# Row means of 16384 rows on one core: how many loads stand ahead of the opening barrier, and which wait the last store carries

## The chip, the core and the metric

The kernel runs on one core of a Trainium2 chip. A core has five engines with an instruction queue each. Four of them matter here: VectorE (DVE in the profile), ScalarE (ACT), GpSimd (POOL) and SyncE (SP), which in this kernel issues every DMA and computes nothing. Sixteen DMA engines move the data; one `dma_start` on 128 partitions is spread over all of them. The engines run on their own and meet only at semaphores. The metric is the device time of one execution in microseconds; lower is better.

## The reference

```
x = np.random.randn(32, 512, 1024).astype(np.float32)
out = (np.sum(x, axis=-1) / 1024.0).astype(np.float32)      # (32, 512)
```

Each of the 32 x 512 = 16384 rows of 1024 numbers is summed and divided by 1024. The input is 67.1 MB, the output 65.5 KB.

## The kernel before

**Tiling.** The 16384 rows are dealt to 128 partitions, 128 rows to each. A partition's rows are in three parts: the first F = 15 rows of the tensor's front (`x_first`), and then M = 97 main rows (`x_main`) and L = 16 last ones (`x_last`), which lie one after the other. One row on all partitions is 128 x 1024 float32, 512 KB.

**Loads.** The list `loads` is made at L99 to L107 and has ten entries, numbered k = 0 to 9 here. Their rows are 2, 16, 16, 16, 16, 16, 15 (main), 15 (first), 10 and 4 (last). Two more DMAs, `pa` and `pb` (L140, L141), bring the last two rows of each partition in unequal halves. Load k goes to buffer `bulk[k % 3]`, of 16 rows each, so there are three buffers, and load k can't be issued before load k - 3 has been consumed.

**The opening.** At L110 the first three loads, which wait for nothing, are issued by SP. `start_loads_at_once` (L15) runs when the program is put together: it takes SP's leading DMAs that carry no wait out of the body and puts them in the first block, ahead of the instruction (a Drain) with which SP joins the first barrier. L113 and L114 close the tile context, and there all engines meet again. Until that barrier opens, no engine gets to the kernel's own instructions, which lie behind a branch (L242).

**The body.** From L130 on SP goes through the other loads in order. Ahead of each it waits until VectorE (`by_dve`), ScalarE (`by_act`, where it has a share) and the earlier load into the same buffer are done (L134 to L137). It then issues the two halves of the last rows and the stores of `res` and `res0` (L143, L145), for which GpSimd has to scale the sums first (L152, L156). VectorE sums whole loads with one `reduce_sum` each (L189); of the loads for the last rows it sums row by row (L180). ScalarE takes 4, 6, 4 and 1 rows of the last four loads and the first row of `pa` (L164).

**The end.** SP waits for VectorE's count and ScalarE's count (L203, L204), and stores the last sums, `fin` (L205). Then it waits for the two other stores, clears the semaphores, and waits for the last store to land (L211). Of the two waits ahead of the last store one is an instruction of its own, and the other is carried by the DMA instruction: in the program before, SP first waits for ScalarE alone, and the store carries the wait for VectorE.

Of the kernel before, what the change touches and what calls it, by code (L numbers as in the profile page):

```python
# [35 lines left out]
def kernel(  # L36
# [6 lines left out]
    nc = tc.nc  # L43
# [36 lines left out]
    loads = []  # L80
    sems = {}

    def sem(name):
        sems[name] = nc.alloc_semaphore(name)
        return sems[name]
# [4 lines left out]
    dve, act, pool = sem("by_dve"), sem("by_act"), sem("by_pool")  # L90
# [8 lines left out]
    for part, src, dst, by in (  # L99
# [3 lines left out]
        for rows, on_act in part:  # L103
            t, s, slot = bulk[n % 3][:, :rows, :], in_bulk[n % 3], n
# [2 lines left out]
            j += rows  # L107


    for t, s, src, *_ in loads[:3]:  # L110
        i = nc.sync.dma_start(out=t, in_=src).then_inc(s, 16)  # L111
        tc.no_tile_sem_insts.add(i.ins.name)
    tc.close()  # L113
# [14 lines left out]


    for k, (t, s, src, on_act, dst, by, slot) in enumerate(loads):  # L130
        if k < 3:
            continue
        if slot is not None:
            nc.sync.wait_ge(dve, done_dve[k - 3])  # L134
            if done_act[k - 3]:
                nc.sync.wait_ge(act, done_act[k - 3])
            nc.sync.wait_ge(s, arrived[k] - 16)  # L137
        nc.sync.dma_start(out=t, in_=src).then_inc(s, 16)  # L138
# [10 lines left out]
    k = len(main) - 1  # L149
# [9 lines left out]
    a = 0  # L159
# [40 lines left out]
    d += 1  # L200


    nc.sync.wait_ge(dve, d)  # L203
    nc.sync.wait_ge(act, a)  # L204
    nc.sync.dma_start(out=o_last, in_=fin).then_inc(landed, 16)  # L205
    for s in (out_first, out_main):
        nc.sync.wait_ge(s, 16)
# [39 lines left out]
```

## Time and profile before

| what | value |
|---|---|
| device time, median of 3 runs (lowest, highest) | 160.44 us (160.39, 160.65) |
| the profiled execution: its own time | 160.87 us |
| the profiled execution: its span | 159.5 us |
| bytes moved, mean rate over the span | 67.18 MB, 421 GB/s |
| DMA queue's time, as a share of 16 engines' span | 98.1% |
| VectorE busy | 116.6 us (73%) |
| ScalarE busy | 18.5 us (12%) |
| GpSimd busy | 1.0 us |

The span runs from the first instruction of the profiled execution, which is SP's first DMA issue, to the last. The 1.4 us between the span and the execution's own time lie outside the kernel's instructions. A DMA packet is counted in the stretch in which it starts, so in short stretches the DMA's rate can read zero while all 16 engines are in the middle of a packet. The waits that end idle time are worked out from semaphore events.

### The profile page before, as it was taken

How to read it: one execution, taken by the hardware profiler on the slowest of the kernel's cores; microseconds unless marked ns; L12 is line 12 of the kernel's file. 1: busy time of each engine (PE TensorE's matmuls, PEld its weight loads, DVE VectorE, ACT ScalarE, POOL GpSimd, SP SyncE). 2: the span in 40 equal slices, each digit the busy share in tenths (PEclk: the TensorE clock that was granted, in tenths of full speed). 3: DMA queues.
4: the chain of work that ended last, by engine and by line, in shares of the span. 5: the costliest groups of instructions: out<-in, count | busy, mean ns of one | idle time of the engine just before them, and what ended most of it. 6: DMA issues, size and time to landing. Idle time of an engine off the chain costs nothing.

```text
span 159.5 us, 141 instructions
## 1 busy us (share of the span) xinstructions
DVE 116.6 (73%) x30; ACT 18.5 (12%) x33; POOL 1.0 (1%) x7
## 2 busy tenths in 40 slices
DVE  0500009999499994999949998599979990399475
ACT  3000000000000000000000000000009100392384
POOL 0000000000000000000000000000000001000000
DMA  8996996996996996998969969998997999798994
GB/s 310 479 526 279 509 526 263 526 526 263 526 526 263 526 493 296 526 427 361 526 296 493 526 263 526 493 385 354 493 493 308 431 493 493 329 462 359 423 396 150
DMA packets 2160, 67.18 MB, mean 421 GB/s; under 512 B 624, under 2 KB 624, under 8 KB 880
## 3 DMA queue, kind: packets, MB, share of 16 engines
q1 hardware_dynamic: 2160, 67.18, 98.1%
HBM read 67.11 MB, written 0.07 MB: 421 GB/s over the span
## 4 chain that ended last, share of the span: by engine, by line
DMA 67%; DVE 29%; another core or an unknown queue 1%; ACT 1%; SPq 1%; issue 0%
DMA bulk<-in_x_dram 52%; DVE res L189 29%; DMA pa<-in_x_dram 15%; ACT junk L164 1%; SPq L111 1%; SPq L138 0%
## 5 line engine op out<-in xcount | busy, mean ns | idle before, releaser
L189 DVE TENSOR_REDUCE res<-bulk 128x16 f32<-128x16384 f32 (+3 forms) x8 | 110.0, 13753 | 37.8 <-DMA bulk<-in_x_dram 37.8
L164 ACT ACTIVATE junk<-bulk 128x1024 f32<-128x1024 f32 x15 | 15.2, 1012 | 136.4 <-DMA bulk<-in_x_dram 136.4
L180 DVE CUSTOM_DVE_ANT_0 bulk<-bulk 128x512 f32<-128x512 f32 x9 | 5.7, 689 | 3.4 <-DMA bulk<-in_x_dram 3.4
L164 ACT ACTIVATION_READ_ACCUMULATOR junk<-bulk 128x1 f32 x15 | 2.8, 186 | 0.0
L164 ACT ACT_TABLE_LOAD x1 | 1.3, 1283 | 2.4 <-PEq L114 2.4
L152 POOL TENSOR_SCALAR res<-res 128x97 f32<-128x97 f32 x1 | 0.5, 467 | 129.3 <-DVE res L189 129.3
L164 ACT ACTIVATE junk<-pa 128x1024 f32<-128x1024 f32 x1 | 1.0, 1028 | 0.7 <-DMA pa<-in_x_dram 0.7
L180 DVE DVE_READ_ACCUMULATOR2_ANT fin<- 128x1 f32 x10 | 0.8, 83 | 0.0
L180 DVE CUSTOM_DVE_ANT_0 pb<-pb 128x257 f32<-128x257 f32 x1 | 0.4, 428 | 0.3 <-DMA pb<-in_x_dram 0.3
L180 DVE CUSTOM_DVE_ANT_0 pa<-pa 128x256 f32<-128x256 f32 x1 | 0.4, 424 | 0.0
L156 POOL TENSOR_SCALAR res<-res 128x15 f32<-128x15 f32 x1 | 0.3, 264 | 15.7 <-DVE res L189 15.7
L164 ACT ACTIVATION_READ_ACCUMULATOR junk<-pa 128x1 f32 x1 | 0.2, 186 | 0.0
L148 POOL MEMSET pb<- 128x2 f32 x1 | 0.1, 99 | 2.0 <-POOLq L114 2.0
L228 POOL MEMSET const-bfloat16-1.0<- 128x1 bf16 x1 | 0.1, 101 | 0.0
L228 POOL MEMSET const-uint8-127<- 128x1 uint8 x1 | 0.1, 101 | 0.0
L228 POOL MEMSET const-float32-0.0<- 128x1 f32 x1 | 0.1, 99 | 0.2 <-issue 0.2
L228 POOL MEMSET const-float32-1.0<- 128x1 f32 x1 | 0.1, 98 | 0.0
L180 DVE DVE_READ_ACCUMULATOR2_ANT pb<- 128x1 f32 x1 | 0.1, 81 | 0.0
## 6 DMA issues: line engine op xcount, KB each, us to landing
bulk<-in_x_dram SPq DMA_DIRECT2D x2, 7680.0 KB, 39.3
bulk<-in_x_dram SPq DMA_DIRECT2D x1, 5120.0 KB, 31.4
bulk<-in_x_dram SPq DMA_DIRECT2D x1, 2048.0 KB, 23.2
bulk<-in_x_dram SPq DMA_DIRECT2D x1, 1024.0 KB, 4.6
pa<-in_x_dram SPq DMA_DIRECT2D x1, 768.0 KB, 24.7
pb<-in_x_dram SPq DMA_DIRECT2D x1, 256.0 KB, 24.9
bulk<-in_x_dram SPq DMA_DIRECT2D x5, 40.9
out_dram<-res SPq DMA_DIRECT2D x1, 48.5 KB, 24.7
```

What stands on the lines that cost most here:

```text
L111: i = nc.sync.dma_start(out=t, in_=src).then_inc(s, 16)
L148: nc.gpsimd.memset(pb[:, D - c :], 0.0).then_inc(pool)
L152: nc.gpsimd.tensor_scalar_mul(out=res, in0=res, scalar1=scale).then_inc(pool)
L156: nc.gpsimd.tensor_scalar_mul(out=res0, in0=res0, scalar1=scale).then_inc(pool)
L164: nc.scalar.activation(junk[a % len(junk)], src, COPY, scale=by, accum_out=dst).then_inc(act)
L180: return nc.vector.tensor_tensor_reduce(out=src[:, :h], in0=src[:, :h], in1=src[:, h:], scale=by, scalar=0.0, op0=ADD, op1=ADD, accum_out=dst,
L189: nc.vector.reduce_sum(out=dst[:, :m], in_=t[:, :m, :], axis=AX).then_inc(dve)
L228: nc = _bacc.Bacc("TRN2", target_bir_lowering=False, num_devices=1)
```

## The change

The program issues only load 0 (2 rows, 1 MB) ahead of the opening barrier. Loads 1 and 2 (16 rows, 8 MB each) are issued by SP behind it, with no wait of their own. For the loads from k = 3 on the waits are the same as before. At the end SP waits for VectorE by an instruction of its own, and the last store carries the wait for ScalarE.

```
-    for t, s, src, *_ in loads[:3]:
+    for t, s, src, *_ in loads[:1]:
         i = nc.sync.dma_start(out=t, in_=src).then_inc(s, 16)
         tc.no_tile_sem_insts.add(i.ins.name)
     tc.close()
...
     for k, (t, s, src, on_act, dst, by, slot) in enumerate(loads):
-        if k < 3:
+        if k < 1:
             continue
-        if slot is not None:
+        if k >= 3:
             nc.sync.wait_ge(dve, done_dve[k - 3])
             if done_act[k - 3]:
                 nc.sync.wait_ge(act, done_act[k - 3])
...
+    nc.sync.wait_ge(act, a)
     nc.sync.wait_ge(dve, d)
-    nc.sync.wait_ge(act, a)
     nc.sync.dma_start(out=o_last, in_=fin).then_inc(landed, 16)
```

In the order of instructions on each engine only SP's differs: two DMA instructions move from ahead of the barrier and the branch to directly behind them, and the two waits at the end change places.

More of the change, by code (lines that the diff above doesn't have):

```diff
@@ L107 @@
             j += rows
-    for t, s, src, *_ in loads[:3]:
+    for t, s, src, *_ in loads[:1]:
         i = nc.sync.dma_start(out=t, in_=src).then_inc(s, 16)
@@ L130 @@
     for k, (t, s, src, on_act, dst, by, slot) in enumerate(loads):
-        if k < 3:
+        if k < 1:
             continue
-        if slot is not None:
+        if k >= 3:
             nc.sync.wait_ge(dve, done_dve[k - 3])
@@ L200 @@
     d += 1
+    nc.sync.wait_ge(act, a)
     nc.sync.wait_ge(dve, d)
-    nc.sync.wait_ge(act, a)
     nc.sync.dma_start(out=o_last, in_=fin).then_inc(landed, 16)
```

## The prediction

> **What bounds the kernel now.** I read the page first: busy times, the DMA queue's share, the chain of waits. Then I read the time line of the opening and of the end, because the change touches only these.
>
> ```profile
> DVE 116.6 (73%) x30; ACT 18.5 (12%) x33; POOL 1.0 (1%) x7
> q1 hardware_dynamic: 2160, 67.18, 98.1%
> DMA 67%; DVE 29%; another core or an unknown queue 1%; ACT 1%; SPq 1%; issue 0%
> ```
>
> The 16 DMA engines are at work for 98.1% of the span, and no compute engine comes near that. The chain's 29% on VectorE does not make VectorE a bound: its big reductions take 17.22 us but start 19.3 us apart (23.95, 43.28, 62.66), each when its load has landed, and another load is queued meanwhile. So the time is the wait for the first byte, 67.18 MB in a stream without holes, and the work behind the last byte. The change counts only if it moves the first byte, tears a hole in the stream, alters the packets' speed, or lengthens the end.
>
> The opening, from the time line:
>
> ```profile
> 0.00 1.34 SPq L111 DMA_DIRECT2D bulk<-in_x_dram  x3
> 0.32 0.10 POOL L228 MEMSET const-uint8-127<- 128x1 uint8 x1
> 2.40 0.10 POOL L148 MEMSET pb<- 128x2 f32 x1 [1.98 <-POOLq L114]
> 2.40 1.28 ACT L164 ACT_TABLE_LOAD   x1 [2.40 <-PEq L114]
> 4.67 2.29 DVE L189 TENSOR_REDUCE res<-bulk 128x2 f32<-128x2048 f32 x1 [4.67 <-DMA bulk<-in_x_dram]
> ```
>
> SP's three issues begin at 0.00, 0.44 and 0.91 and end at 1.34, while GpSimd's last act ahead of the barrier ends at 0.42: SP comes last to the barrier. Its last barrier step begins at 2.32, and at 2.40 ScalarE and GpSimd work behind it. Load 0 has landed just before 4.67.
>
> The same opening by stretches (columns: stretch, length, busy time of VectorE, ScalarE, GpSimd, clock, DMA share, GB/s):
>
> ```profile
> 0.00:0.90 0.90, 0.00 (x0) 0.00 (x0) 0.19 (x4) 1.00 0.00 0
> 0.90:1.10 0.20, 0.00 (x0) 0.00 (x0) 0.00 (x0) 1.00 1.01 205
> 1.10:2.20 1.10, 0.00 (x0) 0.00 (x0) 0.00 (x0) 1.00 0.92 261
> 2.20:3.80 1.60, 0.00 (x0) 1.28 (x1) 0.10 (x1) 1.00 1.03 430
> 3.85:4.35 0.50, 0.00 (x0) 0.00 (x0) 0.00 (x0) 1.00 5.01 2163
> ```
>
> A packet is counted where it starts; load 0's are 8 KB and load 1's 64 KB. 2163 GB/s for 0.5 us is 1.08 MB, so all 16 engines took their first 64 KB packet of load 1 (1.05 MB) between 3.85 and 4.35. The packet records behind these rows put load 0's first packets at 1.01 (earliest engine) to 1.42 (latest), and load 1's at 3.86 to 4.31, each directly behind load 0 on its engine. Load 1, issued at 0.44, lies untouched until 3.86.
>
> The end:
>
> ```profile
> 157.83 0.19 ACT L164 ACTIVATION_READ_ACCUMULATOR junk<-pa 128x1 f32 x1
> 157.91 0.08 DVE L180 DVE_READ_ACCUMULATOR2_ANT fin<- 128x1 f32 x1
> 158.09 0.33 SPq L205 DMA_DIRECT2D out_dram<-fin  x1
> ```
>
> ScalarE is done at 158.02, VectorE at 157.99, and the store starts at 158.09.
>
> **The change part by part.**
>
> *Load 0.* It is still issued at 0.00 with nothing ahead of it. First byte at 1.01 as before: 0.
>
> *The barrier.* Two issues leave SP's way to it: from the end of the first (0.39) to the end of the third (1.34) is 0.95 us. The other engines are at the barrier by 0.5, so it opens 0.95 earlier: SP's last step begins at 1.37 instead of 2.32. ScalarE's table load and GpSimd's memset start 0.95 earlier too. That is worth nothing: ScalarE's first real work is at 119.86, `pb` is read at 157.2, and VectorE waits for load 0 until 4.67 anyway.
>
> *Loads 1 and 2 behind the barrier.* ScalarE and GpSimd got to their own instructions 0.08 after SP's last step began (2.32 to 2.40); I take the same for SP, so load 1 is issued at 1.45 instead of 0.44 and load 2, one issue of 0.43 and a gap of 0.05 on, at 1.93 instead of 0.91. From issue to first packet load 0 needed 1.01 to 1.42. With that, load 1's packets can start at 2.46 to 2.87. They are wanted at 3.86 to 4.31. Even the latest engine's figure against the earliest want leaves 1.0 us. Load 2 is wanted 19.3 us later. The cover is load 0 itself, 1 MB on the DMA engines until 3.86; without it the delay of 1.01 us (0.44 to 1.45) would stand whole in the time. No row of this trace shows a load appended to the ring so shortly before it runs dry. The nearest is the issue of load 3 at 6.98 into a running stream (64 KB packets beside it keep 2.42 us), which gives 0; the far bound is that the engines begin anew after load 0 and pay 1.01. It can't be below 0, since load 1's packets already follow load 0's without a gap. I take 0, with ends 0 and +1.01. Behind the two moved issues in SP's queue stands load 3 with its wait for VectorE, which ends at 6.96; SP gets there at 2.4, so load 3 and all later issues stay.
>
> *The slow first packets.* From 1.10 to 2.20 the stream ran at 261 GB/s, then at 430: 1.1 x (430 - 261) / 430 = 0.43 us lost. In that stretch the descriptors of loads 1 and 2 are being made, which now happens 1.0 later. If they are what slows the packets, load 0 gains 0.43, unless the disturbance only moves along to 2.4 to 3.4. If it costs as much there and the cold start stays too, the change loses 0.43. The issue at 6.98 speaks for neither: no 64 KB packet beside it is longer than 2.43 against 2.42. I put the slow packets down to a cold start and take 0, with ends -0.43 and +0.43.
>
> *The waits at the end.* Before, SP's own wait instruction for ScalarE ends with the count at 158.02, and the store starts 0.07 later, at 158.09. After, that instruction waits for VectorE (157.99 to 158.00), so the store can start at 158.07, when the carried wait for ScalarE is met: -0.02. Where a wait is carried and nothing else is in the way the DMA starts 0.02 behind the count (131.76 to 131.78 at L138), so if VectorE comes last in some execution, the swap costs 0.05 there. Ends -0.05 and +0.05.
>
> Sum: 0 + 0 + 0 - 0.02 = -0.02. The profiled execution took 160.87 with a span of 159.5, 0.43 above the median of 160.44; by the same sum it would become 160.85. For the median: 160.42.
>
> Two rules speak against the change. The Trainium skill, "Runtime: NRT & Kernel Launch", section Instruction fetch mechanics, says that a taken branch to code outside the two pages at hand forces a fetch before the engine goes on, and loads 1 and 2 now stand behind SP's branch. The trace shows only the program's own DMA queue inside the span, and two engines went on 0.08 us after the barrier, so by the row this is 0; the page gives no price, and by its rule the sum would grow by whatever exceeds the 1.0 of cover. The same skill, "DMA: Bandwidth & Descriptors", section Rules for kernel authors, wants a DMA issued early so that its fixed cost overlaps with other work. By that alone the later issue would cost up to its 1.01 us, 161.4; the row shows the fixed cost still under load 0, and the sum stays.
>
> **The rivals.**
>
> *A hole behind load 0 (slower).* Place: the first passage from load 0 to load 1. It needs load 1's issue later than 3.86 - 1.01 = 2.85, so 1.4 us after 1.45; a loss of 0.32 us (0.2%) needs 3.17. Or it needs the engines to pay part of the 1.01 again because their rings are almost dry. For it: no row shows either case, and SP's way through the branch is not in the trace because SP's next act, at 4.66, is a wait that ends there. Against it: if the barrier opened no earlier than today (2.34), load 1 would be issued at 2.40 and still be in time. Half of the far bound, 0.5, gives 160.9.
>
> *Load 0 runs undisturbed (faster).* The slow stretch of 1.10 to 2.20 goes because the two later loads are no longer being made ready in it: up to 0.43, 160.0. For it: the slow packets end at about the time when load 2's descriptors must be done (0.91 + 1.01 = 1.92). Against it: the packets beside the issue at 6.98.
>
> *All is hidden (the forecast).* What moves lies under load 0, and what is left is 0.02 us.
>
> **How the numbers follow.** 0.2% is 0.32 us, about what a measurement of this kernel can tell from no change; its three runs lie 0.26 apart. The forecast, inside that bound, has 0.60: its margin of 1.0 us is over three times the bound, but two of its four terms rest on rows that are not quite the case. The hole has 0.21, the undisturbed load 0.19. Predicted is 160.42. The low end is the faster rival's full gain and the low run's distance from the median (160.42 - 0.43 - 0.05 = 159.94); the high end is the hole at half its bound with a little over it for the spread, 161.0. A hole of the full 1.01 (161.4) is left out. The likeliest case's own range is 160.2 to 160.7.
>
> **What would show each step right or wrong.** Right: three DMA issues of SP at about 0.00, 1.45 and 1.93; ScalarE's table load near 1.45; the stretch from 3.85 to 4.35 again with all 16 first packets of load 1; VectorE's reductions again near 4.67, 23.95 and 43.28; the store 0.07 to 0.09 behind VectorE's last count. A hole shows as load 0 landing at 4.64 and the reduction of load 1 starting later than 23.95 by its size, with all that follows. The faster rival shows as load 0 landing at 4.2 to 4.4 and everything after it earlier by as much. The prediction is wrong if SP needs over 1.4 us from the barrier to its first issue, if a ring fed with little left in it stalls, or if the stream's own speed changes for a reason that these rows do not show.

## The result: 0.84% slower, and the profile after

The changed kernel takes 161.88 us (median of 6 runs, 161.64 to 162.14) against 160.61 us of the kernel before beside it (160.39 to 160.79). The ratio is 1.0084, with a 95% interval of 1.0074 to 1.0095: 1.27 us slower. The forecast was no change, 160.42, with a range up to 161.0. The profiled execution after took 161.86 with a span of 160.5.

The page of the changed kernel, the lines that answer to those of before (busy times, the DMA queue's share, the chain of waits):

```profile
DVE 116.5 (73%) x30; ACT 18.5 (11%) x33; POOL 1.0 (1%) x7
...
q1 hardware_dynamic: 2160, 67.18, 97.7%
...
DMA 67%; DVE 29%; another core or an unknown queue 1%; ACT 1%; SPq 0%; issue 0%
```

The page hides the loss almost wholly: the DMA queue is at 97.7% instead of 98.1%, and the chain has the same shares. The time line of the opening has it:

```profile
0.00 0.38 SPq L111 DMA_DIRECT2D bulk<-in_x_dram  x1
...
1.44 0.81 SPq L138 DMA_DIRECT2D bulk<-in_x_dram  x2
...
1.44 1.28 ACT L164 ACT_TABLE_LOAD   x1 [1.44 <-PEq L114]
4.63 2.29 DVE L189 TENSOR_REDUCE res<-bulk 128x2 f32<-128x2048 f32 x1 [4.63 <-DMA bulk<-in_x_dram]
25.58 17.22 DVE L189 TENSOR_REDUCE res<-bulk 128x16 f32<-128x16384 f32 x1 [18.67 <-DMA bulk<-in_x_dram]
```

SP issues load 1 at 1.44 and ScalarE starts at 1.44, both as forecast, and load 0 lands at the same time as before (4.63; before 4.67). But load 1 has landed only at 25.58, where it was 23.95: 20.95 us behind load 0 instead of 19.28.

The stretches of the opening of the changed kernel (columns as before: stretch, length, busy time of three engines, clock, DMA share, GB/s):

```profile
1.10:2.20 1.10, 0.00 (x0) 0.76 (x1) 0.10 (x1) 1.00 0.96 268
2.20:3.80 1.60, 0.00 (x0) 0.52 (x1) 0.00 (x0) 1.00 0.99 420
3.85:4.35 0.50, 0.00 (x0) 0.00 (x0) 0.00 (x0) 1.00 4.13 1393
4.35:5.55 1.20, 0.92 (x1) 0.00 (x0) 0.00 (x0) 1.00 0.98 328
5.55:6.80 1.25, 1.25 (x1) 0.00 (x0) 0.00 (x0) 1.00 0.00 0
```

The first two rows are load 0, as before (261 and 430 GB/s). In the third, 1393 GB/s for 0.5 us is 0.70 MB: ten first packets of load 1 (0.66 MB) and some of load 0. Before, all 16 stood here. In the fourth, 328 x 1.2 is 0.39 MB: the other six. The packet records say the rest: the first packets start at 3.93 to 5.41 (before: 3.86 to 4.31) and take 3.13 us on the mean (2.42 before). The ten that start at 3.93 to 4.23, no later than before, are slow as well (2.87 to 3.43), so a slow first packet and a late start are two things. The second ones take 2.57, the third 2.43, and from there the stream is as fast as ever. The engine that started last, at 5.41, is 1.10 later than the last one before, and its packet was 0.50 longer. That makes 1.6 us, which is the delay of load 1's landing (25.56 against 23.92, by the semaphore's last step: 1.64).

The end (time line):

```profile
158.84 0.19 ACT L164 ACTIVATION_READ_ACCUMULATOR junk<-pa 128x1 f32 x1
158.92 0.08 DVE L180 DVE_READ_ACCUMULATOR2_ANT fin<- 128x1 f32 x1
159.08 0.33 SPq L205 DMA_DIRECT2D out_dram<-fin  x1
```

The store follows ScalarE's end (159.03) by 0.05, where it was 0.07.

Of the 1.64 us at load 1's landing, 1.02 are left when `pa` lands (157.86 against 156.84). Part of the missing 0.62 is the profiled execution of before itself: its 61440-byte packets lost 0.33 us per engine late in the stream, which those of the changed kernel did not (0.01). In the kernels below that have no hole and no extra work, `pa` landed at 156.4 to 156.6, so the changed kernel is 1.2 to 1.5 behind those, in line with the 1.27 of the medians.

### The profile page after: what moved, and what is told of

The parts are those of the page before. It is cut to its first block, busy times and chain, and to the rows that moved or that the text cites. A ratio compares the mean times of both kernels' runs of the same rounds, so it can differ in the third digit from the quotient of the medians.

```text
span 160.5 us, 141 instructions
## 1 busy us (share of the span) xinstructions
DVE 116.5 (73%) x30; ACT 18.5 (11%) x33; POOL 1.0 (1%) x7
## 3 DMA queue, kind: packets, MB, share of 16 engines
q1 hardware_dynamic: 2160, 67.18, 97.7%
## 4 chain that ended last, share of the span: by engine, by line
DMA 67%; DVE 29%; another core or an unknown queue 1%; ACT 1%; SPq 0%; issue 0%
DMA bulk<-in_x_dram 51%; DVE res L189 29%; DMA pa<-in_x_dram 15%; ACT junk L164 1%; SPq L138 0%
```

## The experiments

The first theory after the result, called A: load 1's descriptors reach the DMA engines too late. The word lead stands below for the time from the issue of load 1 to the moment when the first DMA engine has finished load 0 and wants more. It was 3.4 us before and is 2.4 in the changed kernel. The gap in the table is the time from VectorE's start on load 0 to its start on load 1, which is 19.3 us in a stream without a hole.

| kernel | load 1 issued at | lead, us | gap, us | ratio to before (95%) |
|---|---|---|---|---|
| before | 0.44 | 3.4 | 19.28 | 1 |
| two loads ahead | 0.43 | 3.4 | 19.30 | 0.9996 (0.9987 to 1.0005) |
| between the barriers | 0.78 | 3.3 | 19.31 | 0.9999 (0.9990 to 1.0008) |
| half way | 1.11 | 2.8 | 20.51 | 1.0065 (1.0045 to 1.0085) |
| changed kernel | 1.44 | 2.4 | 20.95 | 1.0084 (1.0074 to 1.0095) |
| loads moved, waits not swapped | 1.43 | 2.4 | 20.99 | 1.0084 (1.0068 to 1.0100) |
| load 2 late | 1.45 | 2.5 | 21.33 | 1.0109 (1.0092 to 1.0126) |
| load 1 behind load 0's landing | 4.59 | none | 21.72 | 1.0142 (1.0127 to 1.0157) |
| 3 rows, one load ahead | 1.43 | 3.7 | 19.32 | 0.9997 (0.9988 to 1.0006) |
| 4 rows, one load ahead | 1.45 | 5.1 | 19.28 | 1.0008 (0.9999 to 1.0018) |
| 1 row, three loads ahead | 0.43 | 2.2 | 19.38 | 1.0001 (0.9991 to 1.0011) |

**Which half of the change.** First the loads alone, then the waits alone.

```
-    nc.sync.wait_ge(act, a)
     nc.sync.wait_ge(dve, d)
+    nc.sync.wait_ge(act, a)            # the changed kernel with the end of before
```

> Only the loads are moved behind the barrier; the two waits at the end stay as they were. If the loss is made in the opening, as the landing of load 1 at 25.56 instead of 23.92 says: as the changed kernel, 1.0 to 1.4 us slower than before (161.6 to 162.0). If the order of the waits at the end has a part: under 0.1 us of difference to the changed kernel either way.

Measured: 161.92, ratio 1.0084, the whole loss. And the kernel before with the waits swapped:

> Only the two waits at the end change places; the loads stay ahead of the barrier. The store starts 0.02 us earlier, or 0.05 later where VectorE comes last: within 0.1 us of before, no difference that can be measured. Rival: the swap has a part in the loss, +0.2 us or more.

Measured: 160.60, ratio 1.0001 (0.9992 to 1.0010). The waits have no part in it.

**Which load.** Loads 0 and 1 ahead, load 2 behind:

```
-    for t, s, src, *_ in loads[:1]:
+    for t, s, src, *_ in loads[:2]:
...
-        if k < 1:
+        if k < 2:
```

> Loads 0 and 1 ahead of the barrier, only load 2 behind it. Theory A (load 1's descriptors come too late, because its issue to the first packets takes 2.5 to 4.0 us while load 0 keeps the engines busy, not the 1.0 to 1.4 of idle engines): load 2 has 19 us of cover, so the time is that of before within 0.2 us, first packets of load 1 at 3.86 to 4.31 and 2.42 us long. Theory C (two issues in a row behind the barrier disturb each other, or the earlier barrier itself disturbs the stream): part of the loss stays, 0.3 us or more.

Measured: 160.45, ratio 0.9996. All first packets of load 1 start at 3.81 to 4.36 and take 2.42. It is load 1's issue alone; load 2, issued at 1.91 instead of 0.91, costs nothing. The earlier barrier doesn't disturb either: here it opens 0.5 us earlier than before, and in the kernels with 3 and 4 rows below, which lose nothing, as early as in the changed one.

```
+        if k == 2:
+            nc.sync.wait_ge(in_bulk[0], 16)      # in the changed kernel: load 2 after load 0 has landed
```

> As the changed kernel, but load 2 is issued only when load 0 has landed (about 4.65), so that nothing is issued between 1.8 and 4.6. Theory A: load 1 is as late as in the changed kernel, +1.0 to +1.4 us. Theory C (load 2's issue, 0.05 us behind load 1's, is what holds back load 1's descriptors): back to before within 0.3 us, load 1 landing at about 23.9.

Measured: 162.26, ratio 1.0109. The hole stays, so it isn't load 2's issue right behind load 1's that makes it, and theory C falls. This kernel is even 0.3 us slower than the changed one. The intervals just overlap; in the profiled execution its last engine starts at 5.60 and its packet takes 3.26, together 0.53 later than in the changed kernel (5.41 and 2.92). Why stays open.

**Busy engines or a slow start.** The same wait put ahead of load 1:

> Load 1 is issued only when load 0 has landed (about 4.65), into engines that stand idle. Theory A (late because the engines are busy): first packets 1.0 to 1.4 us after the issue, at 5.7 to 6.1, each 2.42 us long; slower than before by 1.8 us (6.1 less 4.3). Theory B (the descriptors of a 16-row load need 2.5 to 4 us by themselves, whatever the engines do): first packets spread over 5.7 to 8.6 and about 3.2 us long; slower by 2.5 to 4 us.

Measured: 162.73, ratio 1.0142, 2.2 us slower: between the two theories. The stretches of this kernel, in the opening of load 1:

```profile
4.40:5.50 1.10, 0.90 (x1) 0.00 (x0) 0.00 (x0) 1.00 0.00 0
5.50:6.00 0.50, 0.50 (x1) 0.00 (x0) 0.00 (x0) 1.00 6.19 2097
6.00:8.40 2.40, 0.89 (x1) 0.00 (x0) 0.00 (x0) 1.00 0.00 0
8.40:9.10 0.70, 0.00 (x0) 0.00 (x0) 0.00 (x0) 1.00 3.47 1498
```

2097 GB/s for 0.5 us is 1.05 MB, 16 packets of 64 KB: on idle engines all 16 start together, 0.96 to 1.34 us after the issue at 4.59 (packet records: 5.55 to 5.93). So theory A's first half holds: on idle engines no start is late. But the second packets come only from 8.44 on. The first took 3.09 us on the mean, the second 2.43. So a load that an engine takes up fresh pays some 0.67 us on its first packet in the drained kernel, much as in the changed one (0.71). Theory A did not have this, and theory B had it for another reason. 1.62 us of later starts (5.93 against 4.31) and 0.67 of slow packets make 2.3; measured 2.2.

**The size of the load.** A load 1 of 2 rows, so that its packets are 8 KB:

```
-    main = [(2, 0)] + [(16, 0)] * 5 + [(15, 4)]
+    main = [(2, 0)] * 2 + [(16, 0)] * 5 + [(13, 4)]      # on the changed kernel
```

> Only load 0 (2 rows) ahead of the barrier; load 1 also has 2 rows, the next 16. Load 1 is issued at about 1.44 and wanted at 3.86 as in the changed kernel, but in packets of 8 KB; load 2 (16 rows) is issued at about 1.9 and wanted at 6.3, a lead of 4.4 us. If the hole comes from the size of the load behind (16 rows, 64 KB packets): under 0.5 us slower than before. If every load that comes with a lead of 2.4 us pays, whatever its size: 0.8 us or more slower.

Measured: 161.94, ratio 1.0088 (1.0071 to 1.0105). From the time line:

```profile
4.66 2.29 DVE L189 TENSOR_REDUCE res<-bulk 128x2 f32<-128x2048 f32 x1 [4.66 <-DMA bulk<-in_x_dram]
...
8.43 2.29 DVE L189 TENSOR_REDUCE res<-bulk 128x2 f32<-128x2048 f32 x1 [1.48 <-DMA bulk<-in_x_dram]
27.76 17.22 DVE L189 TENSOR_REDUCE res<-bulk 128x16 f32<-128x16384 f32 x1 [17.05 <-DMA bulk<-in_x_dram]
```

1 MB needs 2.4 us in the stream; here load 1 lands 3.8 us behind load 0, 1.4 too late, and load 2 is on time again (19.33). The loss is that of the changed kernel within the intervals, so a small load that comes late costs as much as a large one. Eight of its fresh packets of 8 KB took 0.9 to 1.2 us where 0.31 is normal: again about 0.7.

**The lead.** Loads 1 and 2 behind the first barrier but ahead of the two of the tile context:

```
-    first.instructions = first.instructions[:at] + loads + first.instructions[at:]
+    past = ...          # behind SP's wait in the first barrier
+    first.instructions = (first.instructions[:at] + loads[:1]
+        + first.instructions[at:past] + loads[1:] + first.instructions[past:])
```

> Load 0 ahead of the first barrier as in the changed kernel; loads 1 and 2 right behind that first barrier but ahead of the two barriers of the tile context, so load 1 is issued at about 0.75 instead of 0.44 (before) or 1.44 (changed). Theory A (load 1 needs a lead before its first packets are wanted at 3.86; 3.4 us are enough, 2.4 are not, by the two issue times): a lead of 3.1 us lies between them, so 0 to 0.7 us slower than before. Theory D (a load that is issued behind a barrier is slow, whenever that is): as the changed kernel, +1.3 us.

Measured: 160.56, ratio 0.9999. A load behind a barrier isn't slow as such, so theory D falls. From here on theory A has two forms. A1: a fixed lead is needed, between 2.4 and 3.1 us. A2: an issue into running traffic needs about 4.0 us until the last engine has its first packet, and one ahead of the traffic needs less. Then one barrier further:

```
-    first.instructions = first.instructions[:at] + loads + first.instructions[at:]
+    first.instructions = first.instructions[:at] + loads[:1] + first.instructions[at:]
+    close = nc.main_func.blocks[2]
+    past = ...          # behind SP's first wait in this block
+    close.instructions = close.instructions[:past] + loads[1:] + close.instructions[past:]
```

> 2 rows in load 0; loads 1 and 2 are issued between the two barriers of the tile context, load 1 at about 1.1, a lead of 2.8 us and just after load 0's first packets at 1.01. Theory A1: between no loss and that of the changed kernel, and it narrows the needed lead to 2.4 to 2.8 or 2.8 to 3.1. Theory A2: the issue falls into the traffic, last engine at about 1.1 + 4.0 = 5.1, 0.8 late: 0.7 to 1.3 us slower.

Measured: 161.68, ratio 1.0065. The stretches of this kernel:

```profile
3.85:4.35 0.50, 0.00 (x0) 0.00 (x0) 0.00 (x0) 1.00 4.53 1917
4.35:6.20 1.85, 1.63 (x1) 0.00 (x0) 0.00 (x0) 1.00 0.21 71
```

1917 x 0.5 is 0.96 MB, 14 packets of 64 KB and a rest; 71 x 1.85 is 0.13 MB, two. Two engines were late, at 4.67 and 4.81, with first packets of 3.09 and 3.01 us, and two are enough: the 16 steps of load 1's semaphore run from 23.91 to 25.06, and VectorE starts at 25.08, behind the last. So 0.33 us of issue time, from 0.78 to 1.11, turn no loss into most of it.

More cover instead of an earlier issue, with 4 rows in load 0:

```
-    main = [(2, 0)] + [(16, 0)] * 5 + [(15, 4)]
+    main = [(4, 0)] + [(16, 0)] * 4 + [(14, 0)] + [(15, 4)]
```

> Load 0 has 4 rows instead of 2 (and load 5 has 14 instead of 16), all three loads ahead of the barrier. The same bytes in the same stream: within 0.3 us of before by both theories. Load 1 is wanted about 2.4 us later than before, at 6.3.

> Load 0 has 4 rows, and only load 0 stands ahead of the barrier, as in the changed kernel. Load 1 is issued at about 1.44 and wanted at about 6.3, a lead of 4.9 us. Theory A (it is the lead that counts): first packets of load 1 directly behind load 0 and 2.42 us long, the time that of the kernel with 4 rows and three loads ahead, within 0.2 us. Theory D (behind the barrier it is slow, whatever the lead): 1.0 us or more slower than that kernel.

Measured: 160.58 with three loads ahead (ratio 1.0000, 0.9991 to 1.0009) and 160.61 with one (1.0008, 0.9999 to 1.0018). With a lead of 5.1 us the changed order costs nothing that can be told from zero. With 3 rows, `[(3, 0)] + [(16, 0)] * 4 + [(15, 0)] + [(15, 4)]`:

> Load 0 has 3 rows, only load 0 stands ahead of the barrier. Load 1 is issued at about 1.44 and wanted at 5.1 to 5.6, a lead of 3.7 us. Theory A1 (a fixed lead is needed, between 2.4 and 3.1 us): no hole, the time of before within 0.2 us. Theory A2 (an issue into running traffic needs about 4.0 us until the last engine has its first packet, as 5.41 less 1.44 in the changed kernel; one ahead of the traffic needs less): the last engines start at 5.4 to 5.6, up to 0.4 late and with slow first packets, so 0.3 to 1.0 us slower.

Measured: 160.51, ratio 0.9997. All 16 first packets of load 1 are in time:

```profile
5.15:5.80 0.65, 0.00 (x0) 0.00 (x0) 0.00 (x0) 1.00 3.78 1632
5.80:7.50 1.70, 1.40 (x1) 0.00 (x0) 0.00 (x0) 1.00 0.00 0
```

1632 x 0.65 is 1.06 MB, the 16 packets and one small one of load 0. Issued at 1.43, a lead of 3.7 is enough. The loss of 0.3 to 1.0 us that A2 gave with its 4.0 us did not come.

Last the other way round, 1 row in load 0 and all three loads ahead, `[(1, 0)] + [(16, 0)] * 5 + [(16, 4)]`:

> Load 0 has 1 row, and all three loads stand ahead of the barrier, so that no issue is moved and no barrier is crossed. Load 1 is issued at 0.44 and wanted at about 2.6 to 2.9, a lead of 2.2 us. Theory A1: the hole is there without any barrier, about as in the changed kernel: 0.8 to 1.5 us slower than before. Theory A2 (issued ahead of the traffic): the first packets start on time, and at most their slow first packet of 0.7 us is lost: 0 to 0.7 us slower. Theory D (the barrier): no loss.

Measured: 160.62, ratio 1.0001. The stretches:

```profile
2.60:3.10 0.50, 0.00 (x0) 0.50 (x1) 0.00 (x0) 1.00 5.28 2261
3.10:5.00 1.90, 1.22 (x1) 0.57 (x1) 0.00 (x0) 1.00 0.00 0
```

All 16 (1.05 of the 1.13 MB) are in time, though load 1 was issued only 2.2 us earlier. So no fixed lead is needed, and theory A1 falls: the issue at 0.43, ahead of load 0's first packet at 1.01, needed at most 2.2 us; of those just behind it, the one at 1.11 needed more than 2.8, and those at 1.43 to 1.45 more than 2.5 and at most 3.7.

**In the steady stream.** Is it then any running traffic that delays an issue (A2), or only the stream's first microseconds (S)? ScalarE, idle there, was made a clock. It sums row 0 of load 0 into an unused place n times, 1.04 us each, and SP issues load 2 when it is done; loads 0 and 1 stand ahead of the barrier. Load 2 is wanted at 23.2 to 23.8.

```
-    for t, s, src, *_ in loads[:1]:
+    for t, s, src, *_ in loads[:2]:
...
-        if k < 1:
+        if k < 2:
             continue
+        if k == 2:
+            nc.sync.wait_ge(tick, ticks)
...
+    nc.scalar.wait_ge(in_bulk[0], 16)
+    for i in range(ticks):
...
+        nc.scalar.activation(
+            junk[i % len(junk)], bulk[0][:, 0, :], COPY, scale=1.0, accum_out=idle[:, i : i + 1]
+        ).then_inc(tick)
```

"The same" in the first two expectations means the set-up that the third one, for 16 activations, describes.

> The same with 14 activations: load 2 issued at about 19.2, a lead of about 4.1 us. No loss by both theories, within 0.2 us of before; it also shows that the extra activations and the later issue of load 3 cost nothing by themselves.

> The same with 15 activations: load 2 issued at about 20.3, a lead of about 3.1 us. Theory A2: between no loss and 1.1 us, as between the half-way kernel (2.8: a loss) and the one with 3 rows (3.7: none). Theory S: no loss.

> Loads 0 and 1 ahead of the barrier; load 2 is issued when ScalarE has done 16 extra activations of about 1.04 us (it repeats a row of load 0; their sums go nowhere), so at about 21.3. Load 2 is wanted when load 1's last packets end, at about 23.2 to 23.7: a lead of about 2.1 us, in the steady stream, where no packet is slow. Theory A2 (any issue into running traffic needs 2.8 to 3.7 us): a hole as in the changed kernel, 1.0 to 2.0 us slower than before. Theory S (only the first microseconds of the stream are slow to take up a load): 0 to 0.4 us slower.

> 15 activations and one of half a row: load 2 issued at about 21.0, a lead of about 2.3 us, between the issue at 20.29 (lost 0.7 us) and the one at 21.53 (lost 0.4, no more than with the long lead). Theory E (it counts whether the engines still have packets queued behind the running one at the issue; the last packets of load 1 start at 20.8 to 21.2): between the two, 0.3 to 0.8 us slower than before. Theory A2 (a longer time under traffic, only by chance short at 21.53): 1.0 us or more slower.

> 17 activations: load 2 issued at about 22.6, a lead of about 0.7 us, less than the 1.0 to 1.4 us from issue to first packet on idle engines. Both theories: a hole of 0.4 to 0.7 us and slow first packets of up to 0.7 us, 0.7 to 1.5 us slower than before.

And the control, in which load 2 stays ahead and only load 3 waits for 14 activations:

> Loads 0 to 2 ahead of the barrier as before; ScalarE does the 14 extra activations, and only load 3 waits for them (issue at about 19.4 instead of 6.98, wanted at 42.6). If the 0.3 us of the kernels with extra activations come from these or from the late load 3: the same 160.8, 0.2 to 0.4 us slower than before. If they come from load 2's issue into the stream: as before within 0.15 us.

| load 2 issued at | lead, us | load 1 to load 2, us | time, us | ratio to before (95%) |
|---|---|---|---|---|
| ahead (control) | 22.6 | 19.35 | 160.92 | 1.0021 (1.0011 to 1.0031) |
| 19.41 | 3.9 | 19.33 | 160.83 | 1.0019 (1.0009 to 1.0028) |
| 20.29 | 2.9 | 20.35 | 161.30 | 1.0039 (1.0025 to 1.0053) |
| 21.23 | 2.2 | 19.34 | 160.93 | 1.0025 (1.0015 to 1.0035) |
| 21.53 | 1.7 | 19.34 | 160.94 | 1.0018 (1.0009 to 1.0028) |
| 22.51 | 0.8 | 20.73 | 161.90 | 1.0091 (1.0073 to 1.0109) |

The control takes 0.35 us more than the kernel before, without a hole. So that much belongs to the extra activations or to load 3's late issue, and the other rows are read against it. (The kernel with the issue at 19.41 was expected within 0.2 us of before and took 0.27 more; this was the reason for the control.) VectorE's start on load 2, in the control and with leads of 2.9, 2.2 and 0.8 us in this order, each from its own kernel's time line:

```profile
43.45 17.22 DVE L202 TENSOR_REDUCE res<-bulk 128x16 f32<-128x16384 f32 x1 [2.13 <-DMA bulk<-in_x_dram]
```

```profile
44.28 17.22 DVE L202 TENSOR_REDUCE res<-bulk 128x16 f32<-128x16384 f32 x1 [3.14 <-DMA bulk<-in_x_dram]
```

```profile
43.55 17.22 DVE L202 TENSOR_REDUCE res<-bulk 128x16 f32<-128x16384 f32 x1 [2.12 <-DMA bulk<-in_x_dram]
```

```profile
44.75 17.22 DVE L202 TENSOR_REDUCE res<-bulk 128x16 f32<-128x16384 f32 x1 [3.51 <-DMA bulk<-in_x_dram]
```

The idle time ahead of it, 2.1 us in a stream without a hole, is longer with a lead of 0.8, where a hole is expected (0.8 is less than the 0.96 to 1.34 from issue to first packet on idle engines), and not with 2.2 or 1.7. The lead of 2.2 cost 0.36 us over before, inside the range of theory E, but the control has as much and there is no hole, so that is no support for E. A2 falls as it was put: an issue at 21.53, into running traffic, needed at most 1.7 us. But the lead of 2.9 shows a hole again: one engine's first packet took 3.25 us and two others' 2.9, and load 2 landed 1.0 late. Its time lies 0.4 above the control's, with intervals that overlap. So S isn't borne out either.

## Why the prediction was wrong

**What bounds the kernel** was read rightly: a stream that runs at 2.42 us per 64 KB packet, and a change that counts only by a hole. The hole came, and it is the whole loss.

**Load 0, the barrier, the issue times**: right to 0.04 us for load 1 (1.44 for 1.45), the table load (1.44) and VectorE's start on load 0 (4.63 for 4.67). Load 2 came at 1.82 instead of 1.93, because load 1's issue took 0.33 us there and not 0.43; nothing hangs on it. Nor does anything on a small misreading: `pb` is first needed at 156.87 and read at 157.56, not at 157.2. SP went through the branch in 0.08 us (1.36 to 1.44) like the other engines, so the rule of the Trainium skill ("Runtime: NRT & Kernel Launch", Instruction fetch mechanics) on branches, which gives no price, had no part here.

**"From issue to first packet load 0 needed 1.01 to 1.42. With that, load 1's packets can start at 2.46 to 2.87."** This is the step that failed. The figure came from an issue into idle engines, and it holds there (0.96 to 1.34 in the kernel that drains first). Issued at 1.44, just when load 0's first packets are under way, load 1 reached the last engine 4.0 us after its issue (5.41), 4.1 in the kernel that only moves the loads and 3.7 in the half-way one. The 1.0 us of cover that I counted was not there.

**"The nearest is the issue of load 3 at 6.98 into a running stream, which gives 0."** The row was the wrong one for the question. It shows 64 KB packets that keep their 2.42 us beside an issue. It can't show when the issued load is ready, since load 3 is wanted only at 42 us.

**The far bound, +1.01**, was too small for the same term: it had the later start (1.10 measured for the last engine), but not the slow first packet (0.7 us on the mean, 0.50 on that engine). Together they made 1.6 of the 1.64 at load 1's landing; the median lost 1.27. The rival of the hole had the right mechanism and place, and stated the case "rings almost dry"; its price of 0.5, half of that bound, was the mis-sized number, and its chance of 0.21 too low.

**The slow first packets of load 0** remain in the changed kernel (268 GB/s from 1.10 to 2.20, for 261). There loads 1 and 2 are issued at 1.44 and 1.82, inside that stretch, so this alone doesn't decide. The kernel in which load 1 waits for load 0's landing does, because nothing but load 0 is issued in it before 4.59:

```profile
1.10:2.20 1.10, 0.00 (x0) 0.76 (x1) 0.10 (x1) 1.00 0.87 253
```

Load 0 was no faster by itself, and VectorE started on it at 4.60: the faster rival is refuted. The prediction's cold start stays a name for this, not a cause. The same kernel has a slow first packet on a load whose neighbours in memory had just been read, which speaks for the taking up and against the place read first; no run separates the two.

**The end**: right. The store came 0.02 us nearer to ScalarE's end, and the swap alone measures as nothing.

The rule of the Trainium skill on issuing a DMA early ("DMA: Bandwidth & Descriptors", Rules for kernel authors), which I put aside because the row showed the cost covered, spoke rightly against this change; by it alone the prediction had up to 161.4, and 161.88 came.

What stays open: why an issue at 1.11 needs more than 2.8 us and, by its one profile, one at 20.29 more than 2.9, while one at 0.43 needs at most 2.2 and one at 21.53 at most 1.7. One reading, that of theory E, fits all rows: an issue is taken up late when the engines have started on their packets and still have others queued behind the running one. At 1.1 to 1.45 most of load 0 is queued, and at 20.29 load 1's last packet was; at 21.23 and 21.53 most or all of the last packets were running (they start at 20.8 to 21.4), and at 0.43 nothing had started. That is argued from six issue times and not shown, and the traces don't tell which record belongs to which DMA engine.

None of the kernels beat the one before by more than the measurement can tell.

## What to carry to other kernels

The time from a DMA's issue to its first packet on idle engines is not the lead that it needs behind a stream that has just begun: here an issue at 1.1 to 1.45 lost 1.1 to 1.7 us when it came 2.4 to 2.8 us ahead of need, and nothing with 3.7 and more, while issues ahead of the stream's first packet lost nothing with 2.2 and more. So before a load is moved behind a barrier, compare its new lead with a row that shows an issue with so short a lead; if the trace has none, price the late start and the slow first packet together. Where the issue can't be earlier, a larger load ahead of it buys the lead at no cost (1.5 instead of 1 MB here).

## What the runs showed of the hardware

- A load that the DMA engines took up without having had it queued in time paid about 0.7 us per engine on its first packet of 64 KB (3.1 for 2.42 us, changed and drained kernel), and as much on eight first packets of 8 KB (about 1.0 for 0.31). Two late engines out of 16 were enough to delay the whole load (half way: 1.2 us).
- The delay stays: in the changed kernel the landings of the 16 engines are spread over 1.16 us at load 1 and still over 1.15 us at `pa` (0.37 before).
- A shorter lead isn't always worse: in the steady stream 1.7 and 2.2 us lost nothing beside the control, 2.9 us showed a hole of 1.0 us in its profiled execution, and 0.8 us lost 1.0 us.
